# A hybrid encoder layer on one core: two more doubles of the seven-product stage, and the fill of both attentions dealt anew

## The chip, the cores and the metric

One core of a Trainium2 chip runs one launch of one encoder layer in float32. The metric is the time of the launch on the device, in microseconds (us); several runs are taken and their median stands for the kernel. TensorE is PE in the profile, VectorE DVE, ScalarE ACT, GpSimd POOL, and SyncE SP, which here only issues transfers.

## The reference

Sequence 512, width 1024, one layer. Cut to what matters:

```python
x = x + 0.5 * swiglu(rmsnorm(x, n1), w1a, w3a, w2a)          # FFN a, 2816 wide
h = rmsnorm(x, mix_norm)
[A | B | gates] = h @ w_in
# A: dilated window attention, 24 heads of 64 in 3 groups (dilation 1, 4, 16), merged by log-sum-exp
# B: 8 query heads of 128 on 2 key/value heads, normalised per head, rotary, full softmax
merged = sigmoid(gA + b) * (o_A @ w_branch_a) + sigmoid(gB + b) * (o_B @ w_branch_b)
x = x + merged @ w_out
x = x + 0.5 * swiglu(rmsnorm(x, n2), w1b, w3b, w2b)          # FFN b
return rmsnorm(x, final_norm)
```

Accuracy is kept by splitting both factors of a product: a high part H (rounded by ACT) and a rest L (subtracted by DVE). `mm3` (L247) adds HH, HL and LH, so a block of 128 x 128 weights costs three matmuls.

## The kernel before

**Weights.** `order` (L104 to L112) is the list of all weight tiles of 128 x 1024, in the order of their use. `loads` and `prep` (L184, L219) walk it: SP loads a raw tile (wr, or wa, wt, ws in a seven-product stage), ACT casts it to wh (L234), DVE subtracts to wl (L235). Ring buffers (`ring`, L160) bound how far they run ahead.

**The order of the work.** PE's instructions run in the order in which the code issues them; for the other engines a scheduler deals them out from the same program. FFN a comes first, then the mixer: `project_qk` (L739), attention A, attention B, the output projections, and FFN b.

**Head and seven-product stage.** `project_qk` first runs the head: `items` up to ("sw", 0), here the values v1 of attention A (32 steps) and the gates 0 to 3 (8 steps each). A step is three matmuls of 512 columns. Beside it every fourth step from n = 12 issues one of the twelve parts of `tq_steps` (L713), which makes TQ, four combinations of quarters of the activations, split in TQH and TQL. Then `strassen` (L301) runs doubles: four feature blocks of 128 at once (two pairs of queries and keys), with weights and activations cut into 2 x 2 quarters and seven products of quarters (A11, S1, S2, A12, S3, S4, A22) in place of eight. S1 and S3 need sums of raw weights, which POOL's accumulating loads form (L216); S2 and S4 are summed by DVE (L233). Each product is 24 matmuls of 256 columns. There are five doubles for queries and keys (pairs of `PAIRS` 0 to 9) and one for the values v0. Each is evicted by `evict` (L783) and its two halves are stored to DRAM (qk_d) by POOL (L773).

**Fill.** The rest of `items` is a generator of steps (288 here) that the attentions draw from while their own chains run on DVE and ACT: `weave` (L380) takes n fill steps for each number n that the attention yields, `gap` takes n at once, `until` takes steps until an item is done. Attention A has four rounds hp: scores S, exponents, a merge (L903) that scales P, transposes T, values. GAP_F is the fill ahead of the first round, GAP_X the fill ahead of the last values. `fetch` (L706) loads stored query and key tiles back, by POOL; pairs 10 and 11 are made in the fill instead.

**Attention B.** The fill's items b0 to b2 give keys and queries by tokens; `rope` and `turn` (L998, L1017) normalise and rotate them on ACT, DVE and POOL (the power of L406 gives rs). `rope_t(grp, first, gap)` (L1035) transposes four token blocks of a group into a bank Tq, split into qH (ACT) and qL (DVE), with `first` fill steps ahead of the first block and `gap` ahead of each other one. `attn_b` (L1052) then has 38 steps s: a score Sb into a bank of a ring of four that Tq and Tb share, its negative maximum nm (DVE), exp to Pb (ACT), reciprocal lq and the scale of Pb (both DVE, L1066 and L1067); five steps later the transpose Tb of four such Pb, split to PTH (ACT) and PTL (DVE), and one step after that the value product. After each step it draws one fill step (GAP_B), so that the last fill item, pa with 32 steps, lies beside it; ma is pa's result, copied by ACT (L698).

Of the kernel before, what the change touches and what calls it, by code (L numbers as in the profile page):

```python
# [11 lines left out]
F32 = mybir.dt.float32  # L12
F32R = mybir.dt.float32r
AF = mybir.ActivationFunctionType
# [8 lines left out]
PAIRS = ((0, 0), (1, 0), (0, 1), (0, 2), (1, 1), (1, 2), (2, 0), (3, 0), (2, 1), (2, 2), (3, 1), (3, 2))  # L23
NSQ = 10
STEPS = ("A11", "S1", "S2", "A12", "S3", "S4", "A22")
GAP_F = 16
GAP_X = 4
GAP_Y = 4
GAP_V = 6
GAP_S = 6  # L30
GAP_B = 1
LAG = 1
# [37 lines left out]
class Layer:  # L70
    def __init__(self, ctx, tc, a):
# [27 lines left out]
        gates = lambda lo, hi: [("g", j) for j in range(lo, hi)]  # L99
        self.items = ([("v", 1)] + gates(0, 4) + [("sw", 0), ("v", 2)] + gates(4, 6) + [("qk", f) for f in range(NSQ, 12)]  # L100
                      + gates(6, 13) + [("b", g) for g in range(3)] + gates(13, 16) + [("pa", 0)])
        self.head = self.items.index(("sw", 0))
        span = {"v": ("wav", 4), "qk": ("waq", 2), "g": ("wg", 1), "b": ("wb", 4), "pa": ("wpa", 4)}
        self.order = self.ffn_order("a")  # L104
        for kind, n in self.items:
            if kind == "sw":
                self.order += [("swq", at) for at in self.slots(range(0, NSQ + 2, 2))]
                continue
            name, m = span[kind]
            self.order += [(name, m * n + i) for i in range(m)]  # L110
        self.order += [(name, i) for name in ("wpb", "wo") for i in range(8)]
        self.order += self.ffn_order("b")  # L112
        self.raws, self.tiles, self.used, self.wx, self.TQ = {}, [], 0, None, None
        self.cap = len(self.order)
# [5 lines left out]
    def turn_of(self, n):  # L120
        if self.kind[n] != "wt":
            return n
        s, f = self.order[n][0][2], self.order[n][1][0]
        return n - (EARLIER if s != "q" and f >= GROUPS[s][1] else EARLY)

# [34 lines left out]
    def ring(self, tag, n, done, last):  # L160
        held, bufs = self.rings[tag], BUFS[tag]
        pool = self.wb if tag in ("wr", "wh") else self.wx
        if pool is None or (len(held) >= bufs and held[-bufs] >= done):
            return None
        held.append(last)
        if tag[:2] != "wh":
            return pool.tile([128, 1024], F32, tag=tag, name=tag, bufs=bufs)
        at = (self.offset(n) - BASE[tag]) % 256 // 4
        return tuple(pool.tile([128, 1088], F32R, tag=t, name=t, bufs=bufs)[:, at:at + 1024] for t in ("wh", "wl"))
# [18 lines left out]
    def load(self, n):  # L188
# [17 lines left out]
        def part(q):  # L206
            if name[2] == "q" and f == NSQ:
                return self.a["wav0"][2 * int(q[1]) + int(q[2]) - 3].rearrange("p (a c) -> p a c", a=2)
            i, c = 2 * f + int(q[1]) - 1, 512 * (int(q[2]) - 1)
            return w[i:i + 3:2, :, c:c + 512].rearrange("a p c -> p a c")  # L210

# [89 lines left out]
    def strassen(self, s, fs, evict):  # L301
        st, order = {}, self.slots(fs)
        end = self.used + len(order) - 1
        for f, step in order:
# [7 lines left out]
            for j in range(2):  # L312
                for k in range(4):
                    ops = self.right(step, k)
                    if s == "q" and f == NSQ:
# [119 lines left out]
    def ffn(self, s, gin, gnext, hooks, out=None, side=None):  # L435
        with ExitStack() as ctx:
            pool = lambda n, **k: ctx.enter_context(self.tc.tile_pool(name=n, reuse_waits="tile", **k))
            tp = pool("hT", bufs=1, side="right")
            self.TH = tp.tile([128, 3, 4, 256], F32R, name="TH")
            self.TL = tp.tile([128, 3, 4, 256], F32R, name="TL")  # L440
            self.wx = self.shifted(pool("wx", bufs=1), 128)
# [216 lines left out]
    def stream(self, items):  # L658
        nc = self.nc
        for kind, n in items:  # L660
            if kind == "v":
# [9 lines left out]
                yield from self.token("wav", 4 * n, toks, done)  # L671
            elif kind == "qk":
                hp, g = PAIRS[n]
                for part in range(2):

                    def done(ps, hp=hp, part=part, g=g):
                        t = self.qk[hp][part, g] = self.ap.tile([128, T], F32, tag="qk", name="qk", bufs=9)
                        nc.vector.tensor_mul(t.rearrange("p (r m) -> p r m", r=4),
                                             ps.rearrange("p (m r) -> p r m", r=4),
                                             self.acc.rearrange("p (r m) -> p r m", r=4))  # L680

                    yield from self.feat("waq", 2 * n + part, done)
            elif kind == "g":
# [22 lines left out]
    def fetch(self, hp):  # L706
        for f, (h, g) in enumerate(PAIRS[:NSQ]):
            if h == hp:
# [30 lines left out]
    def project_qk(self):  # L739
        nc, tc = self.nc, self.tc  # L740
        with ExitStack() as ctx:
            pool = lambda n, **k: ctx.enter_context(tc.tile_pool(name=n, reuse_waits="tile", **k))
            tp = self.shifted(pool("qT", bufs=1), 64)
            self.TQ = [tp.tile([128, 4, 4, 256], F32R, name=f"TQ{c}") for c in "HL"]
            self.wx = self.shifted(pool("wxq", bufs=1), 64)
            cp, qp = pool("cq", bufs=2), pool("qo", bufs=2)
            steps = self.tq_steps(cp)
            hooks = {7: self.stat_r, 12: self.stat_R, 17: self.stat_p}
            for n, _ in enumerate(self.stream(self.items[:self.head])):
                if n in hooks:  # L750
                    hooks[n]()
                if n > 8 and n % 4 == 0 and steps:
                    steps.pop(0)()
# [17 lines left out]
            def store(f, part, t):  # L771
                i = 2 * f + part
                nc.gpsimd.dma_start(self.qk_d[i:i + 3:2].rearrange("c p n -> p c n"), t.rearrange("p (c n) -> p c n", c=2))  # L773

# [9 lines left out]
            def evict(f, step, ps):  # L784
# [15 lines left out]
                elif step == "S4":  # L800
                    nc.vector.tensor_add(hi, ps, hi)
                    if f == NSQ:
                        tokens(lo, 0, slice(0, 256), False)
# [5 lines left out]
                    store(f, 0, o)  # L809
                elif f == NSQ:  # L810
                    tokens(ps, 0, slice(256, 512), True)
# [6 lines left out]

            for _ in self.strassen("q", range(0, NSQ + 2, 2), evict):
                pass  # L820
# [231 lines left out]
    def attn_b(self, pp):  # L1052
# [4 lines left out]
        def score(h, i):  # L1057
# [8 lines left out]
            nc.vector.reciprocal(lq, lq)  # L1066
            nc.vector.tensor_scalar(p, p, lq, None, op0=ALU.mult)  # L1067
            P[h, i] = p
# [18 lines left out]
        for s in range(37 + LAG):  # L1087
# [5 lines left out]
            if pend and t > 0:  # L1093
                value()
            yield GAP_B
        assert not pend

    def mixer(self):
# [7 lines left out]
        with tc.tile_pool(name="oA", bufs=1, reuse_waits="tile") as oa:  # L1106
            self.oH = [oa.tile([128, T], F32R, name=f"oH{h}") for h in range(4)]
            self.oL = [oa.tile([128, T], F32R, name=f"oL{h}") for h in range(4)]
            with tc.tile_pool(name="A", bufs=1, reuse_waits="tile") as ap:
# [7 lines left out]
                for hp in range(4):  # L1117
                    if hp == 3:
                        self.until(fill, ("qk", 11))
                    res = []  # L1120
# [12 lines left out]
            with tc.tile_pool(name="B", bufs=1, reuse_waits="tile") as bp:  # L1133
                self.qH = bp.tile([128, 8, T], F32R, name="qH")
                self.qL = bp.tile([128, 8, T], F32R, name="qL")
                with tc.tile_pool(name="KV", bufs=1, reuse_waits="tile") as kv:
# [4 lines left out]
                    with tc.tile_pool(name="Bp", bufs=1, reuse_waits="tile") as b2:  # L1141
# [6 lines left out]
                        self.until(fill, ("b", 2))  # L1148
                        self.weave(self.rope_t(2, 6, 4), fill)
                    self.wx = None  # L1150
# [168 lines left out]
```

## Time and profile before

| | |
|---|---|
| runs | 1254.65 us median of three (1252.33, 1254.65, 1255.08) |
| the profiled execution | 1252.48 us, span 1250.7 us |
| granted TensorE clock | 0.998 of full speed |
| busy share | PE 99%, DVE 71%, ACT 48%, POOL 10% |
| moved by DMA | 183.49 MB, 147 GB/s on average |

The span is the time from the first to the last instruction. PE is the engine that TensorE's matmuls keep busy; its busy time is not the same as work at its peak, so below the distance from the start of one matmul to the start of the next is used. Times in a timeline are us from the span's start.

### The profile page before, as it was taken

The numbers are of one execution on the slowest core, as the hardware profiler recorded it, in microseconds if no ns is written. First come the engines' busy times: TensorE is split into PE (matmuls) and PEld (weight loads), VectorE is DVE, ScalarE is ACT, GpSimd is POOL, SyncE is SP. The second block draws the span as 40 slices with busy tenths as digits, with TensorE's granted clock in tenths as the row PEclk, the third lists the DMA queues.
The fourth block names the chain that finished last, engine by engine and source line by source line (L and its number), as shares of the span: only waits on it lengthen the run. The fifth ranks groups of instructions, "written<-read, shape, count | busy, mean of one in ns | idle before, by whom it ended". The sixth has DMA issues, their size and how long they took to land.

```text
span 1250.7 us, 20135 instructions
## 1 busy us (share of the span) xinstructions
PE 1239.0 (99%) x8076; PEld 1112.9 (89%) x8076; DVE 891.4 (71%) x1344; ACT 595.6 (48%) x886; POOL 122.6 (10%) x128
## 2 busy tenths in 40 slices
PE   9999999999999999999999999999999999999997
PEld 7897999899898999978888878888889989988997
DVE  7784688468784887567745898866678747874874
ACT  8551365245463444454423546654475425532553
POOL 1111101000210210200000200000301001100001
PEclk9999999999999999999999999999999999999999
DMA  9875777241486882762242220157737536743222
GB/s 299 229 193 166 194 194 197 87 119 55 148 209 190 226 236 87 228 186 78 84 141 88 81 93 18 34 155 233 218 101 189 166 101 185 187 151 107 63 85 68
DMA packets 85981, 183.49 MB, mean 147 GB/s; under 512 B 12528, under 2 KB 19072, under 8 KB 85888
## 3 DMA queue, kind: packets, MB, share of 16 engines
q1 hardware_dynamic: 68048, 141.27, 33.7%
q0 software_dynamic: 17120, 40.39, 16.1%
q8 instruction: 63, 1.03, 0.3%
q10 hardware_dynamic: 720, 0.55, 0.1%
q14 instruction: 30, 0.25, 0.1%
HBM read 170.55 MB, written 15.29 MB: 149 GB/s over the span
## 4 chain that ended last, share of the span: by engine, by line
PE 97%; DVE 1%; ACT 1%; DMA 0%; issue 0%; SPq 0%; POOL 0%; DVEq 0%
PE mm L249 25%; PE mm L251 24%; PE mm L250 24%; PE Y L250 4%; PE Y L249 4%; PE Y L251 4%; PE X L250 2%; PE X L251 2%; PE X L249 2%; PE mm L937 1%; PE S L861 1%; PE Tb L1073 1%; PE T L948 1%; PE Sb L251 1%; PE Sb L250 1%; PE Sb L249 1%
## 5 line engine op out<-in xcount | busy, mean ns | idle before, releaser
L234 ACT CAST wh<-wr 128x1024 fp32r<-128x1024 f32 x139 | 145.9, 1049 | 194.7 <-PE mm L250 125.7
L235 DVE TENSOR_TENSOR wl<-wr,wh 128x1024 fp32r<-128x1024 f32 x139 | 169.6, 1221 | 51.5 <-ACT wh L234 51.2
L249 PE MATMUL mm<-hH,wh 128*128 128x256 f32 (+1 forms) x600 | 198.2, 330 | 0.0
L251 PE MATMUL mm<-hH,wl 128*128 128x256 f32 (+1 forms) x600 | 195.4, 326 | 1.0 <-DVE wl L235 1.0
L250 PE MATMUL mm<-hL,wh 128*128 128x256 f32 (+1 forms) x600 | 195.5, 326 | 0.3 <-DVE hL L389 0.3
L249 PE MATMUL mm<-gg,wh 128*128 128x512 f32 (+1 forms) x376 | 141.5, 376 | 0.0
L250 PE MATMUL mm<-gg,wh 128*128 128x512 f32 (+1 forms) x376 | 141.0, 375 | 0.0
L251 PE MATMUL mm<-gg,wl 128*128 128x512 f32 (+1 forms) x376 | 141.0, 375 | 0.0
L251 PEld LDWEIGHTS mm<-hH,wl 128*128 128x128 f32 x600 | 112.9, 188 | 11.8 <-DVE wl L235 1.4
L249 PEld LDWEIGHTS mm<-hH,wh 128*128 128x128 f32 x600 | 112.8, 188 | 11.7 <-issue 1.0
L250 PEld LDWEIGHTS mm<-hL,wh 128*128 128x128 f32 x600 | 113.0, 188 | 10.4 <-DVE hL L389 0.8
L234 ACT CAST wh<-wa 128x1024 fp32r<-128x1024 f32 x50 | 52.6, 1052 | 102.1 <-PE mm L250 55.4
L234 ACT CAST wh<-wt 128x1024 fp32r<-128x1024 f32 x50 | 52.6, 1052 | 71.1 <-PE mm L250 46.4
L235 DVE TENSOR_TENSOR wl<-wt,wh 128x1024 fp32r<-128x1024 f32 x50 | 61.2, 1224 | 33.1 <-ACT wh L234 32.4
L234 ACT CAST wh<-ws 128x1024 fp32r<-128x1024 f32 x50 | 52.6, 1052 | 66.6 <-PE mm L250 47.5
L249 PE MATMUL mm<-TH,wh 128*128 128x256 f32 x304 | 83.9, 276 | 0.0
L250 PE MATMUL mm<-TL,wh 128*128 128x256 f32 x304 | 83.9, 276 | 0.0
L251 PE MATMUL mm<-TH,wl 128*128 128x256 f32 x304 | 83.9, 276 | 0.0
L249 PEld LDWEIGHTS mm<-gg,wh 128*128 128x128 f32 x376 | 70.6, 188 | 14.1 <-PE mm L251 0.9
L251 PEld LDWEIGHTS mm<-gg,wl 128*128 128x128 f32 x376 | 70.6, 188 | 12.9
L250 PEld LDWEIGHTS mm<-gg,wh 128*128 128x128 f32 x376 | 70.6, 188 | 12.6
L545 DVE TENSOR_TENSOR u<-mm,R 128x512 f32<-128x512 f32 x40 | 27.7, 691 | 75.7 <-PE mm L251 75.5
(270 smaller groups left out, 3210.0 us busy)
## 6 DMA issues: line engine op xcount, KB each, us to landing
wr<-in_w2a SPq DMA_DIRECT2D x22, 512.0 KB, 3.4
wr<-in_w2b SPq DMA_DIRECT2D x22, 512.0 KB, 3.5
wt<-in_w13b SPq DMA_DIRECT2D x20, 512.0 KB, 3.5
wa<-in_w13b SPq DMA_DIRECT2D x20, 512.0 KB, 3.3
wt<-in_w13b POOLq DMA_DIRECT2D x20, 512.0 KB, 6.0
wt<-in_w13a SPq DMA_DIRECT2D x18, 512.0 KB, 3.5
wt<-in_w13a POOLq DMA_DIRECT2D x18, 512.0 KB, 6.1
wa<-in_w13a SPq DMA_DIRECT2D x18, 512.0 KB, 3.4
```

The source lines that it names most:

```text
L234: self.nc.scalar.copy(H, raw)
L235: self.nc.vector.tensor_sub(L, raw, f32(H))
L249: mm(out, lH, rH, start=start, stop=False, skip_group_check=more)
L250: mm(out, lH, rL, start=False, stop=False, skip_group_check=more)
L251: mm(out, lL, rH, start=False, stop=stop, skip_group_check=more)
L545: nc.vector.tensor_mul(u, ps, R)
L861: nc.tensor.matmul(*args, start=True, stop=True)
L937: nc.tensor.matmul(oc, v, p, start=st, stop=sp)
L948: nc.tensor.transpose(ps[:, 128 * b:128 * b + 128], P[h][:, c0 + 128 * b:c0 + 128 * b + 128], self.ident)
L1073: nc.tensor.transpose(pt[:, 128 * j:128 * j + 128], P[h, j][:, 128 * k:128 * k + 128], self.ident)
```

## The change

Gates 0 to 3 leave the head and become the seventh of eight places in the seven-product stage (FG = 12), queries and keys of pairs 10 and 11 leave the fill and become the sixth (NSQ = 12); the values v0 come last (FV = 14). The head is v1 alone, 32 steps, with one part of `tq_steps` every second step from n = 8. The gates' double reads its weights from `wg` and stores to gate_d, by POOL. The fill is 256 steps: v2, gates 4 to 13, b0 to b2, gates 14 and 15, pa. GAP_F is 10 for 16, GAP_X 3 for 4, rope_t(2, 6, 4) becomes rope_t(2, 3, 4). `attn_b` draws a fill step after each step up to s = 25 and after odd steps from then on. Half of the softmax scales (odd i) go from DVE to ACT. `fetch` reads all twelve pairs, and the wait for pair 11 ahead of the fourth round is gone. The loads of raw tiles of that stage are allowed one place ahead of its first tile (`turn_of`, `ring`).

```diff
-NSQ = 10
+NSQ, FG, FV = 12, 12, 14
+HEAD_G = 4
-GAP_F = 16
-GAP_X = 4
+GAP_F = 10
+GAP_X = 3
-GAP_B = 1
+GAP_B = 26
...
-        self.items = ([("v", 1)] + gates(0, 4) + [("sw", 0), ("v", 2)] + gates(4, 6) + [("qk", f) for f in range(NSQ, 12)]
-                      + gates(6, 13) + [("b", g) for g in range(3)] + gates(13, 16) + [("pa", 0)])
+        self.items = ([("v", 1), ("sw", 0), ("v", 2)] + gates(HEAD_G, 14) + [("b", g) for g in range(3)] + gates(14, 16) + [("pa", 0)])
...
-                self.order += [("swq", at) for at in self.slots(range(0, NSQ + 2, 2))]
+                self.order += [("swq", at) for at in self.slots(range(0, FV + 2, 2))]
...
-        return n - (EARLIER if s != "q" and f >= GROUPS[s][1] else EARLY)
+        if s == "q":
+            return max(n - EARLY, self.index["swq", (0, "A11")] - 1)
+        return n - (EARLIER if f >= GROUPS[s][1] else EARLY)
...
-        if pool is None or (len(held) >= bufs and held[-bufs] >= done):
+        s = self.order[n][0]
+        if pool is None or s[:2] == "sw" and tag != "wh" and s[2] != self.stage or (len(held) >= bufs and held[-bufs] >= done):
...
-            i, c = 2 * f + int(q[1]) - 1, 512 * (int(q[2]) - 1)
-            return w[i:i + 3:2, :, c:c + 512].rearrange("a p c -> p a c")
+            src, i = (self.a["wg"], 0) if name[2] == "q" and f == FG else (w, 2 * f)
+            i, c = i + int(q[1]) - 1, 512 * (int(q[2]) - 1)
+            return src[i:i + 3:2, :, c:c + 512].rearrange("a p c -> p a c")
...
-        for f, (h, g) in enumerate(PAIRS[:NSQ]):
+        for f, (h, g) in enumerate(PAIRS):
...
-                if n > 8 and n % 4 == 0 and steps:
+                if n > 6 and n % 2 == 0 and steps:
...
-                i = 2 * f + part
-                nc.gpsimd.dma_start(self.qk_d[i:i + 3:2].rearrange("c p n -> p c n"), t.rearrange("p (c n) -> p c n", c=2))
+                dst, i = (self.gate_d, part) if f == FG else (self.qk_d, 2 * f + part)
+                nc.gpsimd.dma_start(dst[i:i + 3:2].rearrange("c p n -> p c n"), t.rearrange("p (c n) -> p c n", c=2))
...
-            nc.vector.tensor_scalar(p, p, lq, None, op0=ALU.mult)
+            if i % 2:
+                nc.scalar.activation(p, p, AF.Copy, scale=lq)
+            else:
+                nc.vector.tensor_scalar(p, p, lq, None, op0=ALU.mult)
...
-            yield GAP_B
+            yield s < GAP_B or s % 2
...
-                    if hp == 3:
-                        self.until(fill, ("qk", 11))
...
-                        self.weave(self.rope_t(2, 6, 4), fill)
+                        self.weave(self.rope_t(2, 3, 4), fill)
```

The other lines of the diff replace the index of the last double (NSQ by FV), take the kind "qk" out of the fill's generator, and note which stage's buffers are open. In the changed kernel's lines L239 is L235 of before, L1043 is L1050, L1055 is L1062, L1059 is L1066, L1063 is L1067, L158 is L156 and L1058 is L1065; L1061 is the new scale on ACT.

What the change does to the order is seen at the start of attention B. On DVE, before, from the rotation of the last token block to the first maxima nm of the scores (qL is the rest of a transposed query block, z a gate, wl a weight tile's rest):

```order
L1032 TENSOR_TENSOR xk<-xb,xa 128x4x64
L1029 TENSOR_TENSOR xa<-xk,GC_6575 128x512
L1030 TENSOR_TENSOR xb<-xk,GS_6576 128x512
L1050 TENSOR_TENSOR qL<-Tq,qH 128x4x128
L1031 TENSOR_TENSOR xk<-xa,xb 128x4x64
L1032 TENSOR_TENSOR xk<-xb,xa 128x4x64
L687 TENSOR_TENSOR z<-mm,R 128x512
L235 TENSOR_TENSOR wl<-wr,wh 128x1024
L1050 TENSOR_TENSOR qL<-Tq,qH 128x4x128 x2
L687 TENSOR_TENSOR z<-mm,R 128x512
L235 TENSOR_TENSOR wl<-wr,wh 128x1024
L1050 TENSOR_TENSOR qL<-Tq,qH 128x4x128
```

And in the change, the same stretch from the last product of the rotation on:

```order
L1023 TENSOR_TENSOR xb<-xk,GS_6904 128x512
L239 TENSOR_TENSOR wl<-wr,wh 128x1024
L1024 TENSOR_TENSOR xk<-xa,xb 128x4x64
L1025 TENSOR_TENSOR xk<-xb,xa 128x4x64
L1043 TENSOR_TENSOR qL<-Tq,qH 128x4x128
L680 TENSOR_TENSOR z<-mm,R 128x512
L1043 TENSOR_TENSOR qL<-Tq,qH 128x4x128
L239 TENSOR_TENSOR wl<-wr,wh 128x1024
L1043 TENSOR_TENSOR qL<-Tq,qH 128x4x128
L680 TENSOR_TENSOR z<-mm,R 128x512
L239 TENSOR_TENSOR wl<-wr,wh 128x1024
L1043 TENSOR_TENSOR qL<-Tq,qH 128x4x128
```

Three weight rests wl stand there where two stood, the first of them ahead of the last two rotation steps and the last ahead of the fourth qL.

Some rows further up on DVE, before: the reduce of the fourth token block (L1011), the multiply of the third by its rs (L1028), the mean ms of the fourth, from which POOL makes rs, and the two products of the third:

```order
L1011 TENSOR_REDUCE ss<-sqb 128x4
L1028 TENSOR_TENSOR xk<-xk,rs 128x512
L405 TENSOR_SCALAR ms<-ss 128x4
L1029 TENSOR_TENSOR xa<-xk,GC_6575 128x512
L1030 TENSOR_TENSOR xb<-xk,GS_6576 128x512
```

And in the change:

```order
L1021 TENSOR_TENSOR xk<-xk,rs 128x512
L1004 TENSOR_REDUCE ss<-sqb 128x4
L1022 TENSOR_TENSOR xa<-xk,GC_6903 128x512
L409 TENSOR_SCALAR ms<-ss 128x4
L1023 TENSOR_TENSOR xb<-xk,GS_6904 128x512
```

The reduce and the mean stand behind one long row more each.

On ACT, before, from the first exp of attention B on (L1065 is exp, L156 the split of a transposed Pb):

```order
L1065 ACTIVATE Pb,lq<-Sb,nm 128x512 x4
L234 CAST wh<-wr 128x1024
L1065 ACTIVATE Pb,lq<-Sb,nm 128x512
L156 CAST PTH<-Tb 128x512
L1065 ACTIVATE Pb,lq<-Sb,nm 128x512
L156 CAST PTH<-Tb 128x512
```

And in the change:

```order
L1058 ACTIVATE Pb,lq<-Sb,nm 128x512 x3
L1061 ACTIVATE Pb<-Pb,lq 128x512
L1058 ACTIVATE Pb,lq<-Sb,nm 128x512
L691 COPY ma_7669<-mm 128x512
L1058 ACTIVATE Pb,lq<-Sb,nm 128x512
L1061 ACTIVATE Pb<-Pb,lq 128x512
L1058 ACTIVATE Pb,lq<-Sb,nm 128x512
L158 CAST PTH<-Tb 128x512
L1061 ACTIVATE Pb<-Pb,lq 128x512
L158 CAST PTH<-Tb 128x512
```

The scale of the fourth Pb, the second row of L1061, stands behind five exp and a copy of ma; the cast of a weight tile that stood there is gone from these rows.

## Rows read from the trace of the kernel before

**Rows 1.** The page: busy time of the engines, and the chain that ended last.

```profile
PE 1239.0 (99%) x8076; PEld 1112.9 (89%) x8076; DVE 891.4 (71%) x1344; ACT 595.6 (48%) x886; POOL 122.6 (10%) x128
...
PE 97%; DVE 1%; ACT 1%; DMA 0%; issue 0%; SPq 0%; POOL 0%; DVEq 0%
```

**Rows 2.** Waits of PE, whole span: us in total, times, longest.

```profile
PE warm L1193 <- POOL R L94: 1.3, 1, 1.3
```

**Rows 3.** Timeline of PE, head: start, duration, engine, line, out<-in; gates, then first products.

```profile
371.71 0.39 PE L249 MATMUL mm<-hH,wh 128*128 128x512 f32 x1
...
393.50 0.28 PE L249 MATMUL mm<-hH,wh 128*128 128x256 f32 x1
...
396.33 0.28 PE L249 MATMUL Y<-TQH,wh 128*128 128x256 f32 x1
```

**Rows 4.** Timeline of PE, the same product of two doubles in a row.

```profile
415.47 0.28 PE L249 MATMUL mm<-TQH,wh 128*128 128x256 f32 x1
...
434.51 0.28 PE L249 MATMUL mm<-TQH,wh 128*128 128x256 f32 x1
```

**Rows 5.** Timeline of DVE, end of the head.

```profile
368.53 1.23 DVE L735 TENSOR_TENSOR TQL<-Traw,TQH 128x1024 fp32r<-128x1024 f32 x1
...
371.59 1.23 DVE L235 TENSOR_TENSOR wl<-wr,wh 128x1024 fp32r<-128x1024 f32 x1 [0.69 <-ACT wh L234]
372.73 0.75 DVE L667 TENSOR_SCALAR V<-mm,r 128x512 f32<-128x512 f32 x1
```

**Rows 6.** Window 406.5 to 468.7: length, busy PE, PEld, DVE, ACT, POOL, clock, DMA share, GB/s.

```profile
406.50:468.70 62.20, 62.20 (x551) 62.20 (x550) 53.37 (x58) 29.05 (x33) 12.17 (x13) 1.00 0.86 232
```

**Rows 7.** Timelines of POOL and PE: fetch and first scores of attention A.

```profile
509.19 4.29 POOL L711 DMA_DIRECT2D qk<-qk_d  x8 [9.59 <-PE mm L251]
...
520.21 1.94 PE L861 MATMUL S<-qk 64*128 64x256 f32 x20
```

**Rows 8.** Timelines of DVE and PE: scales and transposes of the last round of attention A.

```profile
615.86 4.16 DVE L926 TENSOR_SCALAR P<-P,F 128x256 f32<-128x256 f32 x16
...
623.32 1.69 PE L948 MATMUL T<-ident,P 128*128 128x128 f32 x14
```

**Rows 9.** Timeline of PE, start of attention B: first Sb, first Tb, first value.

```profile
733.49 0.48 PE L249 MATMUL Sb<-kH,qH 128*128 128x512 f32 x1
...
741.85 0.33 PE L1073 MATMUL Tb<-ident,Pb 128*128 128x128 f32 x1 [0.15 <-DVE Pb L1067]
...
744.70 0.50 PE L250 MATMUL mm<-PTL,vH 128*128 128x512 f32 x1 [0.46 <-DVE PTL L157]
```

**Rows 10.** Timeline of DVE ahead of and at the start of attention B.

```profile
725.33 0.69 DVE L1028 TENSOR_TENSOR xk<-xk,rs 128x512 f32<-128x512 f32 x1 [0.30 <-POOL rs L406]
...
734.39 0.69 DVE L1050 TENSOR_TENSOR qL<-Tq,qH 128x512 fp32r<-128x512 f32 x1 [0.56 <-ACT qH L1049]
735.00 0.68 DVE L1062 TENSOR_REDUCE nm<-Sb 128x1 f32<-128x512 f32 x1
...
736.72 0.49 DVE L1067 TENSOR_SCALAR Pb<-Pb,lq 128x512 f32<-128x512 f32 x1
```

**Rows 11.** Timeline of ACT, an exp of attention B and the split behind it.

```profile
741.43 0.68 ACT L1065 ACTIVATE Pb<-Sb,nm 128x512 f32<-128x512 f32 x1
...
742.22 0.59 ACT L156 CAST PTH<-Tb 128x512 fp32r<-128x512 f32 x1
```

**Rows 12.** Groups by line of ACT, 300 to 830: busy, mean ns | idle before.

```profile
L721 ACT ACTIVATE Traw<-x,par 128x512 f32<-128x512 f32 x8 | 5.3, 715 | 1.1 <-DVE TQL L735 1.1
...
L397 ACT ACTIVATE sq<-x 128x512 f32<-128x512 f32 x7 | 4.3, 617 | 0.0
```

**Rows 13.** Waits of ACT, 744 to 810: us in total, times, longest.

```profile
ACT PTH L156 <- PE Tb L1073: 20.5, 24, 1.3
```

**Rows 14.** Timeline of PE, two values one step of attention B apart.

```profile
754.55 0.48 PE L249 MATMUL mm<-PTH,vH 128*128 128x512 f32 x1
...
757.07 0.48 PE L249 MATMUL mm<-PTH,vH 128*128 128x512 f32 x1
```

More of the change, by code (lines that the diff above doesn't have):

```diff
@@ L99, in __init__ @@
         gates = lambda lo, hi: [("g", j) for j in range(lo, hi)]
-        self.items = ([("v", 1)] + gates(0, 4) + [("sw", 0), ("v", 2)] + gates(4, 6) + [("qk", f) for f in range(NSQ, 12)]
-                      + gates(6, 13) + [("b", g) for g in range(3)] + gates(13, 16) + [("pa", 0)])
+        self.items = ([("v", 1), ("sw", 0), ("v", 2)] + gates(HEAD_G, 14) + [("b", g) for g in range(3)] + gates(14, 16) + [("pa", 0)])
         self.head = self.items.index(("sw", 0))
-        span = {"v": ("wav", 4), "qk": ("waq", 2), "g": ("wg", 1), "b": ("wb", 4), "pa": ("wpa", 4)}
+        span = {"v": ("wav", 4), "g": ("wg", 1), "b": ("wb", 4), "pa": ("wpa", 4)}
         self.order = self.ffn_order("a")
@@ L112, in __init__ @@
         self.order += self.ffn_order("b")
-        self.raws, self.tiles, self.used, self.wx, self.TQ = {}, [], 0, None, None
+        self.raws, self.tiles, self.used, self.wx, self.TQ, self.stage = {}, [], 0, None, None, None
         self.cap = len(self.order)
@@ L206, in part @@
         def part(q):
-            if name[2] == "q" and f == NSQ:
+            if name[2] == "q" and f == FV:
                 return self.a["wav0"][2 * int(q[1]) + int(q[2]) - 3].rearrange("p (a c) -> p a c", a=2)
-            i, c = 2 * f + int(q[1]) - 1, 512 * (int(q[2]) - 1)
-            return w[i:i + 3:2, :, c:c + 512].rearrange("a p c -> p a c")
+            src, i = (self.a["wg"], 0) if name[2] == "q" and f == FG else (w, 2 * f)
+            i, c = i + int(q[1]) - 1, 512 * (int(q[2]) - 1)
+            return src[i:i + 3:2, :, c:c + 512].rearrange("a p c -> p a c")
         if step[0] == "A":
@@ L314, in strassen @@
                     ops = self.right(step, k)
-                    if s == "q" and f == NSQ:
+                    if s == "q" and f == FV:
                         ops = [t[:, 128 * j:128 * j + 128] for t in ops] + [t[:, 256 * k:256 * k + 256] for t in cur]
@@ L440, in ffn @@
             self.TL = tp.tile([128, 3, 4, 256], F32R, name="TL")
-            self.wx = self.shifted(pool("wx", bufs=1), 128)
+            self.wx, self.stage = self.shifted(pool("wx", bufs=1), 128), s
             self.cp = self.shifted(pool("c", bufs=2), 128)
@@ L671, in stream @@
                 yield from self.token("wav", 4 * n, toks, done)
[L672 to L682, printed above, removed]
             elif kind == "g":
@@ L744, in project_qk @@
             self.TQ = [tp.tile([128, 4, 4, 256], F32R, name=f"TQ{c}") for c in "HL"]
-            self.wx = self.shifted(pool("wxq", bufs=1), 64)
+            self.wx, self.stage = self.shifted(pool("wxq", bufs=1), 64), "q"
             cp, qp = pool("cq", bufs=2), pool("qo", bufs=2)
@@ L801, in evict @@
                     nc.vector.tensor_add(hi, ps, hi)
-                    if f == NSQ:
+                    if f == FV:
                         tokens(lo, 0, slice(0, 256), False)
@@ L809, in evict @@
                     store(f, 0, o)
-                elif f == NSQ:
+                elif f == FV:
                     tokens(ps, 0, slice(256, 512), True)
@@ L817, in evict @@
                     store(f, 1, o)
-            for _ in self.strassen("q", range(0, NSQ + 2, 2), evict):
+            for _ in self.strassen("q", range(0, FV + 2, 2), evict):
                 pass
```

## The prediction

> **What bounds the kernel now.** I read the page first: PE is busy 1239.0 us, 99% of the span, and the chain of work that ended last is PE for 97% [rows 1]. DVE has 71%, ACT 48%. The list of PE's waits has eight entries, the longest 1.3 us [rows 2], the shortest the 0.15 at 741.85 [rows 9], about 5.5 us in all. So time is the amount of PE's work, plus whatever waits a change creates; there are hardly any waits to remove. The reader should see that a saving on DVE, ACT or a queue is worth nothing by itself, and that only places where PE comes close to waiting matter.
>
> The head's four gates are 4 x 24 matmuls of 512 columns, from 371.71 to 393.50 [rows 3]: 21.79 us, 0.227 us a matmul. A double of the seven-product stage is seven products of 24 matmuls of 256 columns; two starts of the stage's pattern lie 19.04 us apart [rows 4], 2.72 us a product and 0.113 us a matmul, half. So seven products against eight blocks is a saving of one eighth of PE's time, with nothing lost in the pitch.
>
> **The work on PE.** Removed: the head's four gates, 21.79 us [rows 3]; and the four feature blocks of pairs 10 and 11 in the fill, which are as many matmuls of the same shape, 21.8 us. Together 43.6 us. Added: two doubles, 2 x 19.04 = 38.1 us [rows 4]. **Term 1: -5.5 us.** Everything else that the change does moves work; its cost is what PE then waits for.
>
> **The head.** Without the gates the seven-product stage begins at about 371.7 instead of 393.5. Its second product S1 is due one product later, about 374.4, and needs TQ split and its weights split. Now DVE ends the last TQ split at 368.53 + 1.23 = 369.8 [rows 5], and the gates then give it 22 us more. In the change the steps of TQ come every second step from n = 8, so that this split ends nearly as early (my estimate, with one sum of weights more ahead of it, is 370.8), and S1's weight split, once ACT has cast, is done by about 372.8 (a wl holds DVE for 372.73 - 371.59 = 1.14 us [rows 5]). Slack 1.6 us: cost 0. If DVE is later than that, each us is a us of PE (rival D). Gone from DVE there are the four gates' wl; added is one sum of two raw tiles.
>
> **Seven doubles in a row.** The POOL queue gets four more accumulating loads and four more stores, SP loses four gate loads in the head and four gate stores. In 406.5 to 468.7, which is doubles only, DVE is busy 53.37 of 62.20 us, ACT 29.05, the DMA engines 0.86 at 232 GB/s, and PE all of it [rows 6]. More of the same runs at the same rates: cost 0, though 0.86 is the highest DMA share of the stretches that I looked at.
>
> **Attention A.** The gap before its first scores falls from 16 to 10 fill steps; S now starts at 520.21, the eight fetched tiles are issued by POOL from 509.19 on, for 4.29 us [rows 7], and the first scores need only the first two. Starting at about 516 leaves them more than 5 us: 0. The last fetch brings six tiles instead of two (pairs 10 and 11), four issues more on POOL, and nothing but the last scores waits for them: 0, and the price if they came late would be PE standing still from there on. GAP_X 3 brings T of the last pair forward by 0.68: its tiles P are scaled by 615.86 + 4.16 = 620.02, T starts at 623.32 [rows 8]: 3.3 us of cover, 0. Token group b0 now starts before the last values are done; I bound what its accumulator's reuse costs by 0 and one fill step of 0.68 and take 0.
>
> **The start of attention B, the term that decides.** rope_t(2, 3, 4) gives PE three fill steps less ahead of the first Sb than rope_t(2, 6, 4): 3 x 3 x 0.227 = 2.04 us, so PE reaches it at 733.49 - 2.04 = 731.45 [rows 9]. DVE does not get there earlier but later. The order of the instructions shows two things: the reduce of the fourth token now stands behind the multiply of the third and the first of its products, so its POOL power (which DVE waited 0.30 us for at 725.33 [rows 10]) ends 1.20 us later; and three weight splits instead of two stand ahead of the first nm. The first nm was at 735.00, with 0.56 idle shortly before it [rows 10]; it comes at 735.00 + 1.20 + 1.14 - 0.56 = 736.8. What PE meets there: (a) the fourth Sb takes the bank of the fourth Tq, freed when its qL ends, at about 736.8 (0.61 ahead of nm it starts, 0.69 it takes [rows 10]); PE would be there at 731.45 + 3 x 1.4 = 735.7: 1.1 us. (b) The first Tb needs all four Pb. The fourth transpose was due 741.85 - 0.15 - 733.49 = 8.2 us after the first Sb [rows 9]; with (a) that is 731.45 + 8.2 + 1.1 = 740.8. ACT has by its order three exp, a scale, an exp, the copy of ma, an exp and only then the scale that gives the fourth Pb. An exp keeps ACT 0.77 (741.43 to 742.22 [rows 11], with its accumulator's read); nearest to a 512-wide scale from SBUF is the activation of L721, 0.715 us, the other end the squares of L397, 0.617 us [rows 12]; I take 0.66, and 0.62 until the next one. From nm at 736.8 + 0.69: 3 x 0.77, 0.62, 0.77, 0.5, 0.77, 0.66 end at 743.1, so 2.3 us of waiting. What before lost at this place, the 0.46 before the first value and the 0.15 at Tb [rows 9], is part of this wait now: 1.1 + 2.3 - 0.6. **Term 2: about +2.8.** Lower end 0 (if DVE runs ahead as it did), upper end 4.5 (scale at 0.72, nothing of the old waits goes).
>
> Beside (b), the Trainium skill, page "ScalarE: Activation LUTs", Rules for kernel authors, speaks against this edit: it gives multiplications to VectorE, not to ScalarE. The row agrees in kind: the scale took DVE 0.49 us at 736.72 [rows 10], against 0.62 to 0.72 for the ACT rows. With that rule followed (all scales left on DVE) the fourth Pb would be there about 1.0 us sooner and the 0.8 us of the next part would go, so the sum would be about -2.8 in place of the value below.
>
> **The rest of attention B.** Half of the 32 scales move from DVE to ACT. ACT waited for Tb before PTH 24 times, 20.5 us, 0.85 each [rows 13]; a scale of 0.62 on every second step fits under that. Where a weight cast of 1.05 falls into the same step it does not: three steps, about 0.3 each. **Term 3: +0.8**, ends 0 and 1.0. The fill is 32 steps shorter and only part of that is taken from the gaps ahead (GAP_F, GAP_X, rope_t), so from s = 26 on every second step has no fill. A step with fill lasts 757.07 - 754.55 = 2.52 us [rows 14], without it 1.84, and in that time Tb, PTH (0.59) and PTL (0.69) have to follow each other for the next value. By the same chain two of these steps wait about 0.35. **Term 4: +0.7**, ends 0 and 1.5. FFN b's weight tiles sit in other buffers by a shift of two in the count, a phase that other stages run without a wait: 0, at most 1.
>
> **Sum.** -5.5 + 2.8 + 0.8 + 0.7 = -1.2 us on the profiled execution of 1252.48: 1251.3. The median of the runs, 1254.65, lies 2.2 above that execution, so **1253.5** beside it. A change of 0.2%, 2.5 us, is about the least that a measurement of this kernel can tell from none.
>
> **Rivals.**
> A. Attention B starts without new waits, because DVE and ACT keep ahead (its idle gaps close when PE comes earlier, and my row-by-row chain is too slow). For it: DVE has 0.30 and 0.56 us idle just there [rows 10], and before lost only some 0.6. Against it: DVE's own order, one weight split more in 2 us less. Term 2 becomes -0.6: -5.5 - 0.6 + 0.8 + 0.7 = -4.6, 1250.0; with terms 3 and 4 also at 0, -6.1, 1248.5. Chance 0.34.
> B. The forecast, most of the eighth given back at the start of attention B: 1253.5, its own range 1252 to 1256. Chance 0.48. With it goes E, that a double is not worth what it says: the first product of the stage took 396.33 - 393.50 = 2.83 us here [rows 3], not 2.72; if the two added doubles ran at that pitch, 14 x 0.11 = +1.5, 1255.0. Chance 0.05, against it [rows 4], which lie in the stage's middle as the added ones do.
> C. Slower: the scales on ACT. If PTH of every second step is held up by the scale before it, the value behind it waits on PE each time: 16 scales. At half a scale each, 16 x 0.31 = 5.0, and 1258.5. It decides from (1.2 + 2.5) / 16 = 0.23 us a scale on. Against it the 0.85 us that ACT waits in such a step [rows 13]. Chance 0.09.
> D. Slower or level: the head. DVE has 16 steps less and the stage needs it at once. It would have to be 1.6 + 1.2 + 2.5 = 5.3 us late to end slower. Against it: the splits were done by 369.8 [rows 5]. Chance 0.04.
>
> **How the numbers follow.** Faster by over 0.2% is A: 0.34. Within 0.2% are B and E: 0.53. Slower are C and D: 0.13. The range reaches over B to the end of A and a little into C and leaves out about 2 in 10: 1248.6 to 1256.8.
>
> **What would show it.** Right: PE busy about 5 us less; doubles 19.04 us apart, seven of them; the first Sb some 2 us closer to the end of b2's tokens; then a wait of PE of about 1 us for qL before the fourth Sb and of about 2 us for Pb in the first Tb, released by ACT's scale; two or three short waits for PTL where ACT casts weights and behind s = 26. Wrong: PE's list of waits no longer than before (then A); waits for PTL in ten or more steps (then C); a wait for wl or TQL in the first two products of the stage (then D); a double of more than 19.2 us (then E).

## The result and the profile after

The changed kernel takes 1257.97 us in the median of five runs (1257.65 to 1259.73), the kernel before 1252.51 in its five (1252.33 to 1255.08). The ratio is 1.0042, with a 95% interval of 1.0031 to 1.0054: **slower by 5.5 us**, where 1253.5 was forecast and nothing above 1256.8 was in the range.

The page of the changed kernel, busy times and the chain that ended last, against [rows 1]; the execution profiled is the slowest of the five, 1259.73 us with a span of 1258.0:

```profile
PE 1240.1 (99%) x8220; PEld 1117.1 (89%) x8220; DVE 904.0 (72%) x1346; ACT 612.9 (49%) x914; POOL 132.7 (11%) x140
...
PE 88%; DVE 5%; ACT 3%; DMA 2%; issue 1%; POOL 0%; SPq 0%; POOLq 0%; DVEq 0%; ACTq 0%
```

PE is as busy as before, although it was given 5.5 us less to do (part of that busy time ran at a lower clock, see the last section); the chain goes through DVE, ACT and transfers for a tenth of the span. The waits of PE in the changed kernel (us in total, times, longest), against [rows 2]:

```profile
PE T L941 <- DVE MX L862: 3.7, 4, 1.8
PE Tb L1069 <- ACT Pb L1061: 1.7, 1, 1.7
PE warm L1187 <- POOL R L95: 1.3, 1, 1.3
...
PE Sb L253 <- DVE qL L1043: 0.7, 1, 0.7
PE mm L254 <- DVE PTL L159: 0.6, 3, 0.2
```

Three of them are the ones forecast for attention B. The first was not: the transposes T of attention A wait for the maxima MX, since T takes a bank that MX frees.

**Where the time went.** Two marks split the span: the first Tq of the last token group, and the first stat of FFN b. The timeline of PE, of the kernel before and then of the changed kernel:

```profile
723.49 0.27 PE L1046 MATMUL Tq<-ident,xk 128*128 128x128 f32 x1
...
911.38 0.28 PE L413 MATMUL stat<-ones,acc 128*128 128x1 f32 x2
```

```profile
729.39 0.27 PE L1039 MATMUL Tq<-ident,xk 128*128 128x128 f32 x1
...
918.74 0.28 PE L417 MATMUL stat<-ones,acc 128*128 128x1 f32 x2
```

Up to the last token group PE has as much to do as before: -21.8 for the gates, +38.1 for the doubles, and 24 fill steps of 0.68 less. By the gates, the doubles and six steps less of GAP_F the first scores should come 12.2 us later; they come at 532.13 for 520.21, 11.9 later, so nothing is lost ahead of attention A. The first mark should have come 2.04 us earlier, by the three steps that rope_t no longer takes; it came 5.90 later. Lost between the first scores and this mark: 5.90 + 2.04 = **7.9 us, in attention A**. Between the marks PE has five fill steps less, 3.4 us, and took 189.35 for 187.89: 1.46 + 3.40 = **4.9 us, in attention B**. With -5.5 of work, 7.3 is the difference of the two spans.

**The stall in attention A.** The second round, timeline of PE (start, duration, in brackets the wait before), in the kernel before and then in the changed kernel:

```profile
548.39 1.97 PE L948 MATMUL T<-ident,P 128*128 128x128 f32 x11 [0.53 <-DVE MX L869]
550.53 0.52 PE L948 MATMUL T<-ident,P 128*128 128x128 f32 x3 [0.17 <-DVE MX L869]
550.80 0.48 PE L249 MATMUL mm<-hH,wh 128*128 128x512 f32 x1
```

```profile
563.71 0.39 PE L255 MATMUL mm<-hH,wl 128*128 128x512 f32 x1
564.43 0.63 PE L941 MATMUL T<-ident,P 128*128 128x128 f32 x4 [0.34 <-DVE P L919]
566.82 1.28 PE L941 MATMUL T<-ident,P 128*128 128x128 f32 x7 [1.76 <-DVE MX L862]
568.27 0.87 PE L941 MATMUL T<-ident,P 128*128 128x128 f32 x3 [0.17 <-DVE MX L862]
568.79 0.78 PE L253 MATMUL mm<-hH,wh 128*128 128x512 f32 x1
569.37 0.63 PE L254 MATMUL mm<-hL,wh 128*128 128x512 f32 x1
569.79 0.63 PE L255 MATMUL mm<-hH,wl 128*128 128x512 f32 x1
...
572.02 0.39 PE L255 MATMUL mm<-hH,wl 128*128 128x512 f32 x1
572.25 0.39 PE L253 MATMUL mm<-hH,wh 128*128 128x512 f32 x1
```

The transposes take from 564.43 to 568.79, 4.37 us, against 2.41 in the kernel before. Behind them the matmuls of 512 columns come 0.43 us apart instead of 0.23, until 571.5, and cost another 1.3. The wait ahead of T is 0.2 shorter than before, so this round loses 3.1 us. Why DVE is late with MX stands further up on DVE, in the same round; the kernel before comes first:

```profile
538.75 0.42 DVE L869 CUSTOM_DVE_ANT_0 P<-S,W 128x256 f32<-128x256 f32 x1
...
541.31 0.17 DVE L906 TENSOR_TENSOR MN<-SO 128x16 f32<-128x16 f32 x1
```

```profile
553.47 0.17 DVE L899 TENSOR_TENSOR MN<-SO 128x16 f32<-128x16 f32 x1 [6.06 <-DMA SO<-d]
...
553.77 1.22 DVE L239 TENSOR_TENSOR wl<-wr,wh 128x1024 fp32r<-128x1024 f32 x1
554.91 0.75 DVE L671 TENSOR_SCALAR V<-mm,r 128x512 f32<-128x512 f32 x1
555.57 1.22 DVE L239 TENSOR_TENSOR wl<-wr,wh 128x1024 fp32r<-128x1024 f32 x1
556.70 0.42 DVE L862 CUSTOM_DVE_ANT_0 P<-S,W 128x256 f32<-128x256 f32 x1
```

The first row of the merge of the round before, a minimum over 16 columns, waits 6.06 us for its data to come back through DRAM; a weight split, an eviction of V and another split, all due meanwhile, stand behind it, and only then the maxima. In the kernel before that row (L906, at 541.31) stood behind the first maxima of this round, and its data were there. In the fourth round DVE is late in another way. The first row of the merge of the third round, in the kernel before and in the changed kernel, and DVE's rows behind it in the changed kernel:

```profile
585.22 0.18 DVE L906 TENSOR_TENSOR MN<-SO 128x16 f32<-128x16 f32 x1 [3.90 <-DMA SO<-d]
```

```profile
606.44 0.17 DVE L899 TENSOR_TENSOR MN<-SO 128x16 f32<-128x16 f32 x1 [6.23 <-DMA SO<-d]
```

```profile
611.94 3.10 DVE L919 TENSOR_SCALAR P<-P,F 128x256 f32<-128x256 f32 x12
614.96 0.68 DVE L970 TENSOR_TENSOR oL<-mm,oH 128x512 fp32r<-128x512 f32 x1
615.56 0.41 DVE L862 CUSTOM_DVE_ANT_0 P<-S,W 128x256 f32<-128x256 f32 x1
...
622.05 1.23 DVE L239 TENSOR_TENSOR wl<-wr,wh 128x1024 fp32r<-128x1024 f32 x1 [2.93 <-ACT wh L238]
623.20 0.42 DVE L862 CUSTOM_DVE_ANT_0 P<-S,W 128x256 f32<-128x256 f32 x1
```

PE computes the first scores from 610.58 on; DVE still scales P. It had 8.8 us between that row and these scores before (585.22 to 594.06) and has 4.1 now: 2.7 less because the four fill steps are gone that the wait for pair 11 had put there, and 1.9 less because the merge's data came back later (16.3 us after the start of the second scores of the third round, 14.3 before). And a weight split that waits for ACT stands ahead of the second maxima. T waits until 624.12; with the lower clock behind it this round loses 5.0 us (0.75 in S, 1.7 and 1.2 up to and in T, 1.3 behind). The two rounds together, 8.1 us (2.6 of them the lower clock), account for the 7.9.

### The profile page after: what moved, and what is told of

It is laid out like the page before. It is cut to its first block, busy times and chain, and to the rows that moved or that the text cites. A ratio compares the mean times of both kernels' runs of the same rounds, so it can differ in the third digit from the quotient of the medians.

```text
span 1258.0 us, 20459 instructions
## 1 busy us (share of the span) xinstructions
PE 1240.1 (99%) x8220; PEld 1117.1 (89%) x8220; DVE 904.0 (72%) x1346; ACT 612.9 (49%) x914; POOL 132.7 (11%) x140
## 4 chain that ended last, share of the span: by engine, by line
PE 88%; DVE 5%; ACT 3%; DMA 2%; issue 1%; POOL 0%; SPq 0%; POOLq 0%; DVEq 0%; ACTq 0%
PE mm L253 22%; PE mm L254 22%; PE mm L255 22%; PE Y L254 4%; PE Y L255 4%; PE Y L253 4%; PE X L254 2%; PE X L255 2%; PE X L253 2%; DMA d<-SO 1%; ACT P L870 1%; DVE P L919 1%; PE Tb L1069 1%; ACT Pb L1058 1%; DVE P L862 1%
## 5 line engine op out<-in xcount | busy, mean ns | idle before, releaser
L238 ACT CAST wh<-wr 128x1024 fp32r<-128x1024 f32 x133 | 139.5, 1049 | 173.5 <-PE mm L254 120.7
L239 DVE TENSOR_TENSOR wl<-wr,wh 128x1024 fp32r<-128x1024 f32 x133 | 163.0, 1226 | 38.3 <-ACT wh L238 38.1
L253 PE MATMUL mm<-hH,wh 128*128 128x256 f32 (+1 forms) x552 | 178.2, 323 | 0.4 <-ACT hH L392 0.4
L255 PE MATMUL mm<-hH,wl 128*128 128x256 f32 (+1 forms) x552 | 175.7, 318 | 1.0 <-DVE wl L239 1.0
L254 PE MATMUL mm<-hL,wh 128*128 128x256 f32 (+1 forms) x552 | 175.6, 318 | 0.3 <-DVE hL L393 0.3
L253 PEld LDWEIGHTS mm<-hH,wh 128*128 128x128 f32 x552 | 104.5, 189 | 9.7 <-ACT hH L392 0.9
L255 PEld LDWEIGHTS mm<-hH,wl 128*128 128x128 f32 x552 | 104.2, 189 | 9.5 <-DVE wl L239 1.4
L254 PEld LDWEIGHTS mm<-hL,wh 128*128 128x128 f32 x552 | 104.4, 189 | 8.2 <-DVE hL L393 0.9
L239 DVE TENSOR_TENSOR wl<-wt,wh 128x1024 fp32r<-128x1024 f32 x54 | 66.1, 1224 | 35.4 <-ACT wh L238 34.7
L239 DVE TENSOR_TENSOR wl<-wa,wh 128x1024 fp32r<-128x1024 f32 x54 | 65.9, 1221 | 25.4 <-ACT wh L238 25.4
L253 PEld LDWEIGHTS mm<-gg,wh 128*128 128x128 f32 x376 | 70.6, 188 | 14.2 <-PE mm L255 0.9
```

What stands on the lines that cost most here:

```text
L238: self.nc.scalar.copy(H, raw)
L239: self.nc.vector.tensor_sub(L, raw, f32(H))
L253: mm(out, lH, rH, start=start, stop=False, skip_group_check=more)
L254: mm(out, lH, rL, start=False, stop=False, skip_group_check=more)
L255: mm(out, lL, rH, start=False, stop=stop, skip_group_check=more)
```

## The experiments

Each kernel was run 5 times (the change, e6), 6 times (e2) or 11 times, beside the kernel before on the same chip (28 runs for e1 to e4, 27 for e5 to e8, 21 for e9 and e10). "A" and "B" are what the one profiled execution lost beyond the kernel before, reckoned from the two marks as above. "In the median" below compares the differences to the kernel before.

| run | median us | before | difference | ratio, 95% | A | B |
|---|---|---|---|---|---|---|
| the change | 1257.97 | 1252.51 | +5.5 | 1.0042 (1.0031 to 1.0054) | 7.9 | 4.9 |
| e1 gap before the last round | 1256.35 | 1252.95 | +3.4 | 1.0026 (1.0017 to 1.0035) | 5.0 | 5.3 |
| e2 GAP_F 16 | 1256.49 | 1252.95 | +3.5 | 1.0028 (1.0016 to 1.0039) | 4.3 | 4.9 |
| e3 both | 1254.27 | 1252.95 | +1.3 | 1.0014 (1.0006 to 1.0023) | 4.4 | 6.2 |
| e4 scales on DVE | 1255.32 | 1252.95 | +2.4 | 1.0018 (1.0009 to 1.0027) | 6.6 | 2.7 |
| e5 merge behind the maxima | 1254.77 | 1252.76 | +2.0 | 1.0014 (1.0005 to 1.0023) | 3.4 | 4.9 |
| e6 all scales on ACT | 1262.37 | 1252.76 | +9.6 | 1.0072 (1.0060 to 1.0085) | 5.8 | 7.8 |
| e7 = e3 + e4, GAP_X 1 | 1251.04 | 1252.76 | -1.7 | 0.9986 (0.9977 to 0.9995) | 1.5 | 3.1 |
| e8 = e5 + e4 | 1253.00 | 1252.76 | +0.2 | 1.0001 (0.9992 to 1.0010) | 3.6 | 2.7 |
| e9 = e7 + e5 | 1252.03 | 1253.06 | -1.0 | 0.9992 (0.9983 to 1.0001) | 2.0 | 2.7 |
| e10 = e7, fill at the start of B | 1251.34 | 1253.06 | -1.7 | 0.9986 (0.9977 to 0.9995) | 1.5 | 3.2 |

A single execution of A varies, since its transfers and the granted clock do: of the 7.9 of the change, 2.6 are the lower clock behind its two stalls, and the same stalls in e4 and e6, and the one that e2 keeps, had none of it. The medians decide.

**e1**, four fill steps ahead of the last round's scores:

```diff
+                    if hp == 3:
+                        gap(4)
                     res = []
```

> The changed kernel with four fill steps put back ahead of the scores of the fourth round of attention A, where the removed wait for pair 11 had left some. Theory O (order): in that round DVE is still scaling P when the scores end, and a weight split that waits for ACT stands ahead of the second maxima; the stall (2.74 - 1.99 of S, 4.59 - 2.87 of fill, 2.66 - 1.45 of T, 5.63 - 4.31 of fill behind it at a lower clock, 5.0 us together) goes, the one of the second round (3.1 us) stays: about 5 us less than the changed kernel. Rival M (memory): T waits because the transfers of the merge and the larger fetch crowd each other; four steps do not change the bytes, so the wait shrinks by at most the 2.7 us that the steps give. Rival B: the loss sits in attention B; no change.

The fourth round's stall of 5.0 us is gone entirely, more than the 2.7 that rival M allowed, and the second round's is there (T 4.12 us). But the four steps make token group b0 begin earlier against the last values, and it met their accumulator: a wait of 1.41 us for oL, which the prediction had bounded by 0.68 and taken as 0. So 2.1 us in the median, not 5; by the median alone rival M would not be out.

**e2**, `GAP_F = 16`:

> The changed kernel with GAP_F 16 again. Theory O: on DVE the merge's first row, which waits 6.06 us for a transfer, no longer stands ahead of V, a weight split and the maxima; the stall of the second round (4.37 - 2.41 of T and 5.61 - 4.27 of fill, 3.1 us) goes, that of the fourth round stays: about 3 us less than the changed kernel. Rival M: the same transfers are on their way in the same 6 us, T waits as before: no change. Rival B: no change.

On DVE the merge stands behind the maxima again, and T takes its old 2.41 us; in the fourth round T waits as in the change (1.58 us), but without the lower clock behind it. 1.9 us in the median, where about 3 was expected.

**e3**, both edits:

> The changed kernel with both gaps put back. Theory O: DVE has in attention A the order of the kernel before, both stalls go, about 8 us less than the changed kernel in a profiled execution, and what is left against the kernel before is -5.5 of work and +4.9 of attention B: -0.6. Rival M: less than half of that. Rival B: no change against the changed kernel.

4.1 us in the median: the two add up, but to half of the 8 expected, just at the edge of what rival M allowed. Neither stall is left in the trace; but in this execution, the slowest of its eleven, the merge's data came late in the third round too (DVE waited 4.61 us for it, and S and T 2.1 us for DVE), and the 1.41 us of e1 are there. B is 1.3 higher than in e2; 0.3 of that is a wait for xk at the last token block and 0.6 one for a weight split at 895.07, the rest is not resolved.

**e4**, all softmax scales on DVE, the changed lines of L1060 to L1063 taken back:

> The changed kernel with all softmax scales on DVE, as before. By the prediction's term 2 the fourth Pb comes about 1.0 us sooner and the short waits for PTL go, 0.6 to 0.8: 1.5 to 2 us less than the changed kernel. Theory O agrees and says that attention A's 8 us stay. Rival B, the scales on ACT are the main loss: 4 us less or more.

B falls from 4.9 to 2.7 in the trace. The waits for PTL where a weight is cast are gone, and the first Tb waits 0.86 us, on DVE now, instead of 1.73. The median fell by 3.1 us, more than the 1.5 to 2 expected. What is beyond B lies in A, which the edit does not touch: T waits there as before (1.76 and 1.58 us), but the clock stayed up behind both.

**e5**, PE's order untouched; in the program only one row of DVE is held back, and the scheduler deals some other rows of DVE and ACT anew around it. `self.mxa` is the last maximum of the first two pairs:

```diff
-        nc.vector.tensor_tensor(MN, SO[:, 0, :, 0:2], SO[:, 1, :, 0:2], op=ALU.min)
+        with self.tc.issue_after(self.mxa.ins):
+            nc.vector.tensor_tensor(MN, SO[:, 0, :, 0:2], SO[:, 1, :, 0:2], op=ALU.min)
```

> The changed kernel, PE's order and all transfers as they are; only on DVE the first row of each merge in attention A is issued behind the maxima of that round's first four banks. Theory O (DVE's order is the cause): nothing that waits for a transfer stands ahead of the maxima any more. The stall of the second round (3.1 us in the profile) goes; in the fourth round the maxima no longer stand behind twelve scales of P, so most of its 5.0 us goes too; T may instead wait for P, by up to 2 us. 4 to 7 us less than the changed kernel in the profile, 3 to 5 in the median. Rival M (the transfers themselves are late, the order only shows it): T waits for P as long as it waited for MX, no change within 1.5 us.

This run decides between the two. The same transposes in e5, timeline of PE:

```profile
564.85 1.97 PE L943 MATMUL T<-ident,P 128*128 128x128 f32 x11 [0.53 <-DVE MX L862]
566.99 0.52 PE L943 MATMUL T<-ident,P 128*128 128x128 f32 x3 [0.17 <-DVE MX L862]
567.26 0.48 PE L253 MATMUL mm<-hH,wh 128*128 128x512 f32 x1
567.58 0.40 PE L254 MATMUL mm<-hL,wh 128*128 128x512 f32 x1
```

T takes 2.41 us and the matmuls behind it run at full pitch. A falls by 4.5 us in the trace, 2.6 of them the lower clock that does not come here, and the median by 3.5, with no matmul and no transfer added or taken away. The rival, that the transfers alone make PE wait, expected no change within 1.5 us and falls: in the second round late transfers are the trigger, and the rows queued behind the one that waits are the cost. Why the merge's data come back later in the changed kernel, and whether the four more tiles of the last fetch have a part in it, no run here shows.

**e6**, all 32 scales on ACT:

> The changed kernel with all 32 softmax scales on ACT. With none on ACT attention B lost 2.7 us against its bare work, with 16 it lost 4.9. If each scale on ACT costs by itself, 32 give about 7, 2.2 us above the changed kernel; if only the start and the steps with a weight cast cost, the first Tb waits one more scale, 0.6, and those steps one scale more: 1 to 2 us. If DVE was the one in need there (the change's side), less than the changed kernel.

B: 2.7, 4.9, 7.8 for 0, 16, 32 scales on ACT. The cost grows, but not scale by scale. The 2.9 us between the changed kernel and this one all arise at the first Tb: PE waits 0.28 and 2.11 us there, so that the fourth transpose comes 1.2 later, and behind it, where the granted clock is 0.57 on average from 750 to 754, PE takes another 1.8 longer than in the changed kernel. From the second value on this kernel loses nothing more; so the second branch of the expectation holds, the start and the steps with a weight cast, with the price of the clock on top. The median rose by 4.2 us against the changed kernel; 2.9 of them are B's.

**e7**, e3 and e4 with `GAP_X = 1`:

> Both gaps put back, all scales on DVE, and GAP_X 1 for 3, so that token group b0 begins two steps later against the last values and no longer meets the accumulator that they hold (1.41 us in the run with both gaps). By the ledger: -5.5 of work, +2.7 in attention B, +0 to 3 in attention A from late transfers of the merge: between -2.8 and +0.2 against the kernel before. Rival M: attention A loses 4 or more whatever the gaps: +1.2 and above.

**This one is faster than both kernels**, 1.7 us below the kernel before, with the whole interval under 1. Its waits of PE:

```profile
PE warm L1186 <- POOL R L95: 1.3, 1, 1.3
PE T L941 <- DVE MX L862: 1.0, 4, 0.5
...
PE Tb L1066 <- DVE Pb L1060: 0.9, 1, 0.9
PE Sb L253 <- DVE qL L1043: 0.7, 1, 0.7
```

**e8**, e5 and e4:

> The order of the merge run and all scales on DVE, gaps as in the change. Theory O: -5.5 of work, +2.7 in attention B, 1 to 3 us left in attention A: -1.8 to +0.2 against the kernel before. Rival M: no better than the run with the scales alone on DVE, +2.4.

Level with the kernel before, and 1.8 us below e5: the 2.2 us of B that e4 showed, less the scatter of A. Against e4, from which it differs by the merge's order alone, it gains 2.1 us. It does not reach e7, because T still waits for the second maxima in three rounds, in the fourth behind eight scales of P and a weight split.

**e9**, e7 with e5's order:

> The run with both gaps and the scales on DVE, and in addition the merge's first row behind the maxima. If the runs of one kernel differ because the merge's transfers come late by more or less (1249.7 to 1252.5 there, 1257.7 to 1259.7 for the changed kernel, 0.9 us apart in the run with the merge's order), the spread shrinks to about 1 us; T then waits 0.96 us behind the maxima in each of three rounds instead of only sometimes, so the median stays within 1 us of the other. If the spread has another cause, it stays at 2 us or more.

1.0 us above e7, as far as expected, but the spread is 1.9 us (1251.35 to 1253.29) and not 1. So what makes runs of one kernel differ is not only the merge's transfers; it stays open.

**e10**, e7 with the fill of attention B dealt to its start:

```diff
-            yield s < GAP_B or s % 2
+            yield 2 if s in (2, 4) else (s < GAP_B or s > 30 and s % 2)
```

> The run with both gaps and the scales on DVE, with two fill steps instead of one after the steps 2 and 4 of attention B, taken from the steps 27 and 29. If what is lost at the start of attention B is DVE's lateness (term 2: 0.7 to 0.8 before the fourth Sb, about 1.0 at the first Tb), two steps of 0.68 cover most of it: 1.2 us less there, and 0 to 0.9 more in the steps without fill; 0.3 to 1.2 us less in all. If the wait there follows PE (a queue behind PE's own rows), no less.

No gain. The wait for qL is gone, the one at Tb stayed (1.0), and the step of the second value took 0.8 us more (0.27 of it a wait for PTL): DVE works through its rows almost without a break there, and PE waits for the next of them, wherever fill is put.

## Why the prediction was wrong

**Right.** Term 1: the doubles start 19.04 us apart in the changed kernel too (393.54 to 488.74 is five of them), so the saving of 5.5 us is there. The head: its S1 starts at 374.50, with no wait. Seven doubles in a row: no wait. Rivals C, D and E did not happen as such. That the measured time lies 0.5 us from C's 1258.5 is chance: three waits for PTL are listed, not sixteen. The sign "PE busy about 5 us less" failed (1240.1 for 1239.0).

**Right in kind, for attention B.** Timeline of PE, its first waits in the changed kernel, against [rows 9]:

```profile
744.70 0.50 PE L253 MATMUL Sb<-kH,qH 128*128 128x512 f32 x1 [0.68 <-DVE qL L1043]
...
750.49 0.33 PE L1069 MATMUL Tb<-ident,Pb 128*128 128x128 f32 x1 [1.73 <-ACT Pb L1061]
```

The first nm starts 15.2 us after the first mark, 15.3 by the prediction's sum. The fourth Sb waits for qL 0.7 where 1.1 was forecast, the fourth transpose for ACT's scale 1.7 where 2.3 was. ACT does its rows in the order that the prediction read:

```profile
747.28 0.72 ACT L1061 ACTIVATE Pb<-Pb,lq 128x512 f32<-128x512 f32 x1
747.90 0.69 ACT L1058 ACTIVATE Pb<-Sb,nm 128x512 f32<-128x512 f32 x1
...
748.56 0.59 ACT L691 COPY ma<-mm 128x512 f32<-128x512 f32 x1
749.02 0.71 ACT L1058 ACTIVATE Pb<-Sb,nm 128x512 f32<-128x512 f32 x1
...
749.70 0.74 ACT L1061 ACTIVATE Pb<-Pb,lq 128x512 f32<-128x512 f32 x1
```

A scale takes 0.72 to 0.74 us, at the upper end of [rows 12], but an exp in a row of exps keeps ACT 0.66 and not 0.77. Less the 0.6 that before lost there, term 2 is about 2 instead of 2.8. Term 3 came out at 1.2 for 0.8: three values of 0.93 to 0.99 where 0.55 is the usual. Term 4 came out at 1.3 for 0.7: three values, not two. Together 4.5 to 4.9 us for the 4.3 forecast. Two figures of these paragraphs do not follow from their own terms: with all scales on DVE the sum is -1.2 - 1.0 - 0.8 = -3.0 and not -2.8, and the two reasons given for term 2's upper end of 4.5 lead to about 3.6.

The Trainium skill, page "ScalarE: Activation LUTs", Rules for kernel authors, which gives multiplications to VectorE (for its speed in bf16), is borne out here in fp32 by e4 and e6: 16 scales moved to ACT cost 2.1 us of B, the next 16 2.9, of which 1.8 go with the lower clock, with DVE's scale at 0.49 us [rows 10] and ACT's at 0.72 to 0.74.

**The step that failed** is the paragraph on attention A, with its "0" for the shorter gap and its "0" for the fetch of the last pair. It asked whether the tiles that attention A fetches would be there in time, and they were. It did not ask what DVE's order becomes when the gap ahead of the first round is six fill steps shorter and the wait for pair 11 goes. With the shorter gap the row that waits for a transfer came to stand ahead of MX, which can be read from the order of the instructions, as the same prediction did for attention B. The wait for pair 11, which the paragraph does not name, had put four fill steps ahead of the fourth scores; they were DVE's time to scale P. And that the merge's data could come back later was not weighed at all. Attention A was also where PE already waited: 0.96 us of the 2.41 of T in the second round of the kernel before are wait and pipeline. In the medians the missed loss is 5.5 + 5.5 - 4.9 = 6.1 us, in the profiled execution, the slowest, 7.9.

The number flatters the forecast. It was built on a median of three runs, 1254.65; beside the change the kernel before ran at 1252.51. The forecast was a change of -1.2 us and the measured one is +5.5, so the miss is 6.7 us and not the 4.5 between 1253.5 and 1257.97.

## What to carry to other kernels

When fill is taken away from a kernel whose matmul engine is full, walk through every place that drew on that fill, and read for each the order of the engines beside it: which row waits for a transfer, and what stands behind it. A wait in the program that seems to serve data (here for pair 11) can be what gives another engine its time. If an in-order engine has a row whose data make a round trip through DRAM, look whether the rows that free the full engine's banks stand ahead of it, and put them there where they do not: that gave 3.5 us (e5) and 2.1 (e8 against e4). Where the gaps already kept them apart it gave nothing (e9, 1.0 us above e7).

## What the runs showed of the hardware that was not expected

After PE had waited, the granted clock fell, but not every time. Windows of the changed kernel in the second round of attention A (length, busy PE, PEld, DVE, ACT, POOL, clock, DMA share, GB/s):

```profile
564.00:568.00 4.00, 1.77 (x12) 1.15 (x11) 4.00 (x22) 0.86 (x3) 0.00 (x0) 1.00 0.50 163
568.00:572.00 4.00, 3.83 (x12) 3.11 (x12) 4.00 (x12) 4.00 (x16) 0.00 (x0) 0.57 0.68 182
```

The same windows of e4, where T waits the same 1.76 and 0.17 us:

```profile
564.00:568.00 4.00, 2.10 (x13) 1.15 (x11) 4.00 (x20) 0.89 (x3) 0.00 (x0) 1.00 0.73 191
568.00:572.00 4.00, 3.83 (x19) 3.19 (x19) 4.00 (x12) 4.00 (x16) 0.00 (x0) 1.00 0.51 143
```

In the changed kernel PE was busy 1.77 of 4 us, and in the next 4 us it was granted 0.57 on average: matmuls 0.43 us apart, which is 1.2 in place of 2.4 GHz, for about 2.7 us. In this execution each of the two long waits cost 1.3 us more than the wait itself. The second round of e1 and the first Tb of e6 (a wait of 2.11) were followed by such a drop too. In e4 the clock stayed at 1.00 behind both stalls, as it did behind the fourth round's 1.58 us in e2; in e5, where T waits 0.53 and 0.17 us, it stays at 1.00 as well. So a long wait can bring the drop or not; what decides is not shown here. The five executions of the changed kernel go with it: the shortest, 1257.65 us, has a mean granted clock of 0.999, the longest, the profiled one, 0.994.

The other surprise is how much small transfers vary. For those of the tiles SO and d that are issued between 540 and 580 us, up to 8 KB each, the trace gives from issue to landing 1.8 us at least, 3.7 in the median and 4.3 at most in the kernel before, and 1.7, 2.8 and 6.1 in e3. Each merge waits for a store and a load that is issued behind it, so that a late one delays the rest: in e3 a store of 8 KB issued at 571.3 took 5.5 us, and the load behind it was issued at 576.8.
